# Second half's norm moved behind the mixers' first dense products, alternating score heads, and plain-pair loads spread over the last block

## The chip, the cores and the metric

The kernel runs on one core of a Trainium2 chip. The metric is device time in microseconds (us), the median of several executions. A profile of one execution says when each engine worked: PE is TensorE (matrix products), PEld its weight loads, DVE VectorE, ACT ScalarE, POOL GpSimd, and SP the engine that issues most DMA transfers. Each engine takes its instructions from its own queue, in a fixed order. Engines wait for each other through semaphores, and the order within a queue is set when the program is built.

## The reference

One layer over a sequence of 1024 tokens with 1024 channels, in 32-bit floats:

```python
x = x + 0.5 * swiglu_ffn(rms_norm(x, norm_ffn1), ffn1_w_in, ffn1_w_out)      # d_ff = 2816
x = x + token_mixer(rms_norm(x, norm_mix), w_in, w_out, ...)
x = x + 0.5 * swiglu_ffn(rms_norm(x, norm_ffn2), ffn2_w_in, ffn2_w_out)
return rms_norm(x, norm_final)

def rms_norm(x, g):  return x * rsqrt(mean(x * x, -1) + eps) * g
# token_mixer: p = u @ w_in, split by columns into four mixers of 256 channels (4 heads of 64):
#   a pooling mixer, HGRN2 and GLA (gated linear attention in chunks of 64), and RWKV-7;
#   their outputs are concatenated and multiplied by w_out.
# RWKV-7 per head, over the tokens t:
#   S = S * w_t - (S kk_t)(kk_t * a_t)^T + v_t k_t^T ;   o_t = S r_t
#   then a group norm over each head's 64 channels of o, a bonus term and a gate
```

## The kernel before

**Tiles and precision.** A tile is 128 channels (partitions) by 512 tokens, so a half `h` of the sequence has 512 tokens, and `x[n, h]` are the 16 tiles of the residual stream (n = 0 to 7; they live in buffers named `gr` and `gg`). A dense product is made of three products of rounded operands: each operand is split in a high part and the rest. `split` makes the high part on ACT (L177, or L180 when a norm's gain is multiplied in) and the low part on DVE (L178, L181). `wload` fetches weights into `wraw` and splits them in the same way into `whi` (ACT, L145) and `wlo` (DVE, L146). The products are issued by L89; `mm`, `pg`, `px`, `pq`, `py`, `po` are PSUM banks.

**Stages.** ffn1_in (to about 470 us), ffn1_out (to 691), the mixers (to 1421), ffn2_in (to 1807), ffn2_out with the final norm (to 2057). A tile framework orders the instructions of each stage by priority, which is by default the order in which they are written; `tc.cur_priority` lowered by `URGENT` = 80 pulls instructions forward.

**ffn1_out and ffn2_out.** `out_seven` multiplies five blocks of channels with seven products per block instead of eight. A block has four quarters `q`, each with new weights. Two of the 22 row blocks of `w_out` are left over: the *plain pair*. In ffn1_out, after the five blocks, `h_tile` loads four tiles of the hidden layer and splits them, four `wload` calls bring the weights, and 16 products follow (half 0, n = 0 to 7, then half 1), each with six matrix products, the update of `x[n, h]` on DVE (L747) and `norm_tile`: it splits the updated tile, times the gain, into `xs` (L180 on ACT, L181 on DVE), squares it (ACT, L211) and adds the square to a sum `o` (POOL, L212).

**Norm of the mixers' input.** `rstd_steps(h)` multiplies the sum of squares with ones (`px<-ones,o`), takes the power -1/2 (DVE L226, POOL L227: `rstok`), and spreads it over the partitions (`px<-ident,rstok`, copied to `rsb`). The dense products can start before, since the row scale is applied to their results.

**Mixers.** `mixers` weaves two kinds of work. A stream of dense jobs (`dense_stream`; for each half `wa`, then `rkv0`, which is the three jobs r, k, v, then `gv` and the others) keeps PE busy. Threads (the norm's `rstd_steps`, constants, four units of RWKV, four group norms, attention levels, gates) yield with a time in us from the table `LAT`; a planner's clock decides after which dense product the next step of a thread is put. That sets PE's order, and each step is traced with lowered priority, so the other engines do it early. Of the attention, the *levels* of HGRN2 alternate PE products `pg<-bdt,gin` with DVE operations (L1542 multiplies, L1547 copies under a mask).

**RWKV units.** A unit has two heads of one half, on partitions 0 to 63 and 64 to 127 of the same tiles. Its scores are 16 products of 64 x 128 by 64 x 128, two instructions each: four groups of four, two groups per head, each group in a bank of `px`, evicted by two masked multiplications on DVE (L1293, L1294). After the unit, `group_norm` (L1387 to L1399) is spawned as a thread.

Of the kernel before, what the change touches and what calls it, by code (L numbers as in the profile page):

```python
# [7 lines left out]
F32 = mybir.dt.float32  # L8
F32R = mybir.dt.float32r
# [7 lines left out]
P = 128  # L17
# [18 lines left out]
           pool=10.0, decay=2.9, rstd=3.0, rstd1=7.0, consts=14.4, rs0=2.8, rs1=4.2)  # L36
# [62 lines left out]
class Thread:  # L99
    def __init__(self, gen, ready=0.0):  # L100
        self.gen, self.ready, self.need = gen, ready, ()


class Trunk:
# [99 lines left out]
    def sumsq_add(self, wk, h, x):  # L204
# [4 lines left out]
        else:  # L209
            t = wk.tile([P, H], F32, name="tmp")  # L210
            nc.scalar.activation(t, x, AF.Square)  # L211
            nc.gpsimd.tensor_tensor(self.sq[h], self.sq[h], t, op=ALU.add)  # L212
# [392 lines left out]
    def out_seven(self, wk, w_out, slot, tmp, blocks, early, acc, after=None):  # L605
# [36 lines left out]
        for i, (b0, nb) in enumerate(blocks):  # L642
# [5 lines left out]
            for q in range(4):  # L648
# [28 lines left out]
                for m, w in zip(self.ORDER7, weights(raw, nb)):  # L677
# [29 lines left out]
                    if last and q == 3 and after is not None:  # L707
                        after(m)
                raw = nraw
            hs = nhs  # L710

    def ffn1_out(self, wk, w_out):
# [17 lines left out]
        def h_tile(f, h):  # L730
# [3 lines left out]

        self.out_seven(wk, w_out, slot, lambda: wk.tile([P, H], F32, name="tmp"),
                       ((9, 2), (1, 2), (3, 2), (5, 2), (7, 2)), (8, 8, 8, 8, 0), acc)
        f0 = 2 * PLAIN
        hs = [[h_tile(f, h) for h in range(2)] for f in (f0, f0 + 1)]
        w = [self.wload([(wo[:, f0:f0 + 2, n * P:(n + 2) * P], 0, None)], 2, 256, 1) for n in range(0, KT, 2)]
        self.norm_new()  # L740
        for h in range(2):
            for n in range(KT):
# [5 lines left out]
                self.norm_tile(wk, "gm", n, h)  # L748

    def ffn2_out(self, wk, w_out):  # L750
# [54 lines left out]
        self.out_seven(wk, w_out, slot, tmp, ((9, 2), (1, 2), (3, 2), (5, 2), (7, 2)), (12, 12, 12, 12, 0), load_acc,  # L805
                       after)
        gf = wk.tile([P, D], F32, name="wrawb", bufs=2)
        nc.scalar.dma_start(gf, self.A["norm_final"].broadcast_to([P, D]))
        self.gf = gf

        def h_tile(f, h):
            t = tmp()
            nc.sync.dma_start(t, self.hd[f, h])
            return self.split(t)

        hp = [[h_tile(f, h) for h in range(2)] for f in (f0, f0 + 1)]
# [65 lines left out]
    def weave(self):  # L882
# [5 lines left out]
        self.threads = [Thread(self.rstd_steps(0), LAT["rs0"]), Thread(self.rstd_steps(1), LAT["rs1"]), Thread(self.ysplit()), Thread(consts, LAT["consts"]), Thread(self.rwkv()), Thread(self.gates())]  # L888
# [26 lines left out]
    def spawn(self, gen, us):  # L915
        self.threads.append(Thread(gen, self.te.clk + us))
# [936 lines left out]
```

## Time and profile before

| | |
|---|---|
| median of three executions | 2061.18 us (2061.09 to 2064.62) |
| the profiled execution | 2059.14 us |
| its span, first to last instruction | 2057.3 us |
| PE / DVE / ACT / POOL busy | 1979.4 / 1541.1 / 964.2 / 442.0 us |
| mean granted PE clock | 0.983 |
| mean DMA rate | 169 GB/s |

A row of an engine's list has the start in us, the duration, the engine, the line of the kernel (L89 is line 89), the operation, what is written and what is read (buffer numbers left out), its shape and how many of the kind follow each other; in square brackets is the idle time before it and what ended it. A row of a group has line, engine, operation and count, then total time and the mean in ns, then idle time in front. A row of stretches has for PE, PEld, DVE, ACT and POOL the busy us with the number of instructions, then the granted PE clock (1.00 is full), the DMA share and GB/s. PE's matrix products overlap each other, so the time that one holds the engine is the distance to the next start.

### The profile page before, as it was taken

Reading aid. Unit: us, or ns where it says so; the run is one execution under the profiler, and the core shown is the slowest. Engines: PE = TensorE matmul, PEld = TensorE weight load, DVE = VectorE, ACT = ScalarE, POOL = GpSimd, SP = SyncE. Lnnn points to the kernel's source line nnn. Section 1 sums busy time; section 2 is a strip of 40 time slices with the busy share of each in tenths; the row PEclk is TensorE's granted clock in tenths of the full one; section 3 lists DMA queues with packets and bytes.
Section 4 is the critical chain, followed back from the end, with each engine's and each line's share of the span. In section 5 each row is a group of like instructions: output and inputs, shape, how many; then the busy total and the mean of one; then the engine's idle time right before and its main releaser. Section 6 shows DMA issues by size and latency. Waiting matters only on the chain. (4 is left out here: it accounts for less than half of the span.)

```text
span 2057.3 us, 29356 instructions
## 1 busy us (share of the span) xinstructions
PE 1979.4 (96%) x10424; PEld 1594.1 (77%) x10424; DVE 1541.1 (75%) x2575; ACT 964.2 (47%) x1801; POOL 442.0 (21%) x449
## 2 busy tenths in 40 slices
PE   7899999999999899989999999999999999999995
PEld 5688888887887678778778787787888887778884
DVE  5868878768878856486576676676978898777786
ACT  7435444544443655343464543444544444444444
POOL 0011110003446602002020010100111222134464
PEclk9999999999999999999999999999999999999998
DMA  8336554457653453333443244655445666786622
GB/s 275 114 93 205 200 189 161 157 186 280 253 203 138 156 159 108 91 92 97 145 147 106 83 140 134 207 172 160 139 162 187 202 211 215 242 289 254 246 89 91
DMA packets 304402, 348.60 MB, mean 169 GB/s; under 512 B 28160, under 2 KB 230240, under 8 KB 304256
## 3 DMA queue, kind: packets, MB, share of 16 engines
q1 hardware_dynamic: 301152, 339.14, 49.8%
q0 software_dynamic: 1664, 4.95, 0.7%
q10 hardware_dynamic: 1440, 2.65, 0.4%
q8 instruction: 82, 1.34, 0.3%
q14 instruction: 64, 0.52, 0.1%
HBM read 234.22 MB, written 112.46 MB: 169 GB/s over the span
## 5 line engine op out<-in xcount | busy, mean ns | idle before, releaser
L89 PE MATMUL mm<-xs,whi 128*128 128x512 f32 x1568 | 521.0, 413 | 10.3 <-ACT xs L177 3.9
L89 PEld LDWEIGHTS mm<-xs,whi 128*128 128x128 f32 x1568 | 287.4, 192 | 81.5 <-issue 8.5
L89 PE MATMUL mm<-xs,wlo 128*128 128x512 f32 x784 | 315.4, 402 | 12.1 <-DVE wlo L146 9.7
L145 ACT CAST whi<-wraw 128x512 fp32r<-128x512 f32 (+1 forms) x192 | 118.1, 620 | 171.7 <-PE mm L89 121.1
L300 ACT CAST whi<-wsum 128x512 fp32r<-128x512 f32 x176 | 108.3, 620 | 179.2 <-PE pq L89 49.4
L89 PEld LDWEIGHTS mm<-xs,wlo 128*128 128x128 f32 x784 | 150.6, 192 | 50.4 <-DVE wlo L146 12.1
L89 PE MATMUL pq<-xs,whi 128*128 128x512 f32 x576 | 181.0, 394 | 2.3 <-ACT xs L177 1.8
L146 DVE TENSOR_TENSOR wlo<-wraw,whi 128x512 fp32r<-128x512 f32 (+1 forms) x192 | 134.3, 707 | 63.2 <-ACT whi L145 51.1
L89 PE MATMUL pg<-xs,whi 128*128 128x512 f32 x560 | 176.9, 395 | 4.7 <-DVE hx L559 2.7
L89 PE MATMUL px<-xs,whi 128*128 128x512 f32 x560 | 175.2, 393 | 1.2 <-DVE xs L178 1.2
L301 DVE TENSOR_TENSOR wlo<-wsum,whi 128x512 fp32r<-128x512 f32 x176 | 121.5, 697 | 28.2 <-ACT whi L300 27.9
L89 PE MATMUL pq<-xe,whi 128*128 128x512 f32 x448 | 139.2, 392 | 0.0
L89 PEld LDWEIGHTS pq<-xs,whi 128*128 128x128 f32 x576 | 108.5, 189 | 27.2 <-ACT xs L177 2.7
L89 PEld LDWEIGHTS pg<-xs,whi 128*128 128x128 f32 x560 | 105.0, 189 | 29.5 <-issue 3.1
L89 PEld LDWEIGHTS px<-xs,whi 128*128 128x128 f32 x560 | 105.2, 188 | 25.9 <-DVE xs L178 2.3
L89 PE MATMUL pq<-xs,wlo 128*128 128x512 f32 x288 | 114.2, 396 | 3.8 <-DVE wlo L301 3.8
L340 POOL TENSOR_TENSOR tmp<-tmp 128x512 f32<-128x512 f32 x22 | 33.1, 1503 | 374.0 <-ACT tmp L330 310.6
L89 PE MATMUL pg<-xs,wlo 128*128 128x512 f32 x280 | 110.3, 394 | 0.0
L89 PE MATMUL px<-xs,wlo 128*128 128x512 f32 x280 | 109.9, 392 | 0.0
L89 PEld LDWEIGHTS pq<-xe,whi 128*128 128x128 f32 x448 | 84.3, 188 | 18.7
L622 ACT CAST whi<-wsum 128x512 fp32r<-128x512 f32 x80 | 49.7, 621 | 95.1 <-PE px L89 25.5
L340 POOL TENSOR_TENSOR gr<-gr 128x512 f32<-128x512 f32 x18 | 36.6, 2031 | 256.7 <-ACT gr L330 198.0
(460 smaller groups left out, 4319.9 us busy)
## 6 DMA issues: line engine op xcount, KB each, us to landing
hs<-hx SPq DMA_DIRECT2D x126, 512.0 KB, 3.4
xs<-hs SPq DMA_DIRECT2D x90, 512.0 KB, 6.5
wraw<-in_ffn_w_in SPq DMA_DIRECT2D x68, 512.0 KB, 4.1
wraw<-in_w_in SPq DMA_DIRECT2D x52, 512.0 KB, 4.1
wrawb<-in_ffn_w_in SPq DMA_DIRECT2D x44, 512.0 KB, 4.6
wraw<-in_ffn_w_out SPq DMA_DIRECT2D x42, 512.0 KB, 3.6
xe<-hs SPq DMA_DIRECT2D x36, 512.0 KB, 7.4
wraw<-in_w_out SPq DMA_DIRECT2D x16, 512.0 KB, 4.1
```

The costliest lines, as they stand in the source:

```text
L89: return self._add(self.nc.tensor.matmul(out, lhsT=lhsT, rhs=rhs, **kw), n * 0.42e-3 if rhs.dtype == F32R else max(n * 1.68e-3, 0.04))
L145: nc.scalar.copy(hi[:, :n], raw[:, sl])
L146: nc.vector.tensor_tensor(lo[:, :n], raw[:, sl], hi[:, :n].bitcast(F32), op=ALU.subtract)
L300: nc.scalar.copy(hi[:, :H], a)
L301: nc.vector.tensor_tensor(lo[:, :H], a, hi[:, :H].bitcast(F32), op=ALU.subtract)
L340: nc.gpsimd.tensor_tensor(kept[5], kept[5], kept[7], op=ALU.add)
L622: nc.scalar.copy(v(hi), src)
```

## The change

It has five parts.

1. *Plain pair, ffn1_out.* `out_seven` calls `late(q)` after each quarter of the last block. There one hidden tile and one piece of weights (256 columns of both row blocks) are fetched and split, with `split` into `xs`, `hx` or `xe` buffers. The four `wload` calls are gone.
2. *Plain pair, ffn2_out.* `late(q)` there fetches and splits one hidden tile per quarter, and the gain of the final norm in the first.
3. *Second half's norm.* In the plain pair `norm_tile` is called for half 0 alone. The first four dense jobs (`wa` and the three of `rkv0`) are wrapped by `with_norm`: after the job's body, two tiles of half 1 go through `norm_tile`, with the squares in `st` buffers and the sum on DVE instead of POOL. After the fourth, `rstd_steps(1)` is spawned (it was a thread from the start).
4. *Scores.* Two visits instead of groups: each has eight products whose heads alternate, one bank for each head.
5. *Group norm.* Threads have a precedence of their own; three of the four group norms get none, so their other engines' work is traced in plain order.

```diff
-            t = wk.tile([P, H], F32, name="tmp")
+            t = self.stile() if wk is None else wk.tile([P, H], F32, name="tmp")
             nc.scalar.activation(t, x, AF.Square)
-            nc.gpsimd.tensor_tensor(self.sq[h], self.sq[h], t, op=ALU.add)
+            (nc.vector if wk is None else nc.gpsimd).tensor_tensor(self.sq[h], self.sq[h], t, op=ALU.add)
...
+                if last:
+                    late(q)
...
+        def late(q):                                   # ffn1_out
+            hs[q // 2].append(h_tile(f0 + q // 2, q % 2))
+            raw = wk.tile([P, H], F32, name="tmp")
+            nc.sync.dma_start(raw.rearrange("p (f c) -> p f c", c=256), wo[:, f0:f0 + 2, 2 * q * P:(2 * q + 2) * P])
+            if q < 3:
+                t = wk.tile([P, 2 * H], F32R, name="hx", bufs=3)
+            else:
+                t = wk.tile([P, 2 * H], F32R, name="xe", bufs=6)
+            hi, lo = self.split(raw, t=t)
+            w.append([(hi[:, f * 256:f * 256 + 256], lo[:, f * 256:f * 256 + 256]) for f in range(2)])
...
-        hs = [[h_tile(f, h) for h in range(2)] for f in (f0, f0 + 1)]
-        w = [self.wload([(wo[:, f0:f0 + 2, n * P:(n + 2) * P], 0, None)], 2, 256, 1) for n in range(0, KT, 2)]
...
-                self.norm_tile(wk, "gm", n, h)
+                if h == 0:
+                    self.norm_tile(wk, "gm", n, h)
...
+        def late(q):                                   # ffn2_out
+            if q == 0:
+                gf = self.gf = wk.tile([P, D], F32, name="wrawb", bufs=2)
+                nc.scalar.dma_start(gf, self.A["norm_final"].broadcast_to([P, D]))
+            t = tmp()
+            nc.sync.dma_start(t, self.hd[f0 + q // 2, q % 2])
+            hp[q // 2].append(self.split(t))
...
+        def with_norm(body, n):
+            def both(w):
+                yield from body(w)
+                for k in (n, n + 1):
+                    self.norm_tile(None, "gm", k, 1)
+                if n == KT - 2:
+                    self.spawn(self.rstd_steps(1), LAT["rs1"])
+            return both
...
+        for i in range(4):
+            self.jobs[i] = (self.jobs[i][0], with_norm(self.jobs[i][1], 2 * i))
...
-        for c2 in range(4):
-            ps = self.px.tile([P, 4, P], F32, name="px")
-            hd = c2 // 2
+        for half in range(2):
+            banks = [self.px.tile([P, 4, P], F32, name="px") for _ in range(2)]
             for i in range(4):
+                for hd, ps in enumerate(banks):
+                    hs = slice(hd * 64, hd * 64 + 64)
+                    te.matmul(ps[:, i], lhsT=bk[hs, 4 * half + i].rearrange("p x t -> p (x t)"),
+                              rhs=rK[hs, 4 * half + i].rearrange("p x t -> p (x t)"), start=True, stop=True)
...
+            if half == 0:
+                yield 2 * LAT["score"]
...
-        self.spawn(self.group_norm(pr, h, O, vt, d2), 0.0)
+        self.spawn(self.group_norm(pr, h, O, vt, d2), 0.0, URGENT if pr and h else 0)
```

The changed file has its lines a little further down: the update L747 is L760 there, the levels' L1542 and L1547 are L1568 and L1573, the group norm's L1387 to L1399 are L1413 to L1425.

The first place is DVE at the end of the plain pair. Before, the first mixer weights (`wlo_6247`, `wlo_6251`, read by job `wa`) stand behind the last updates and splits (`gr`, `gg` are x, `xs` the splits):

```order
L747 SCALAR_TENSOR_TENSOR gg_4324<-mm_6170,gg_4324 128x512
L181 SCALAR_TENSOR_TENSOR xs_6164<-gr_4230,vec_76,xs_6164 128x512
L747 SCALAR_TENSOR_TENSOR gg_4324<-pg_6184,gg_4324 128x512
L181 SCALAR_TENSOR_TENSOR xs_6178<-gg_4324,vec_76,xs_6178 128x512
L146 TENSOR_TENSOR wlo_6247<-wraw_6244,whi_6246 128x512
L146 TENSOR_TENSOR wlo_6251<-wraw_6244,whi_6250 128x512
```

After, DVE at the start of the pair has the same weights (now `wlo_6196`, `wlo_6200`) in the last quarter of the last block, before the first update L760:

```order
L672 SCALAR_TENSOR_TENSOR gr_4322<-pg_5879,gr_4322 128x512
L146 TENSOR_TENSOR wlo_6196<-wraw_6193,whi_6195 128x512
L146 TENSOR_TENSOR wlo_6200<-wraw_6193,whi_6199 128x512
L672 SCALAR_TENSOR_TENSOR tmp_4490<-mm_5878,tmp_4490 128x512
L672 SCALAR_TENSOR_TENSOR gg_4324<-px_5880,gg_4324 128x512
L146 TENSOR_TENSOR wlo_6206<-wraw_6203,whi_6205 128x512
L178 TENSOR_TENSOR xs_5964<-tmp_5962,xs_5964 128x512
L672 SCALAR_TENSOR_TENSOR gr_4322<-pq_5881,gr_4322 128x512
L178 TENSOR_TENSOR xe_5969<-tmp_5967,xe_5969 128x512
L675 TENSOR_TENSOR gr_4322<-gr_4322,tmp_4490 128x512
L760 SCALAR_TENSOR_TENSOR gr_4130<-mm_5972,gr_4130 128x512
```

The weights moved ahead of all 16 updates, and the last splits of hidden tile and weights (`xs_5964`, `xe_5969`) stand among the block's own updates.

DVE at the end of the pair after the change still has the splits of half 1 between the updates, and then the small constants, the last two splits and the mean of the norm (`rstok_6234`):

```order
L760 SCALAR_TENSOR_TENSOR gg_4324<-mm_6131,gg_4324 128x512
L181 SCALAR_TENSOR_TENSOR xs_6421<-gr_4230,vec_76,xs_6421 128x512
L760 SCALAR_TENSOR_TENSOR gg_4324<-pg_6139,gg_4324 128x512
L1048 TENSOR_SCALAR omu_6179<-vec_76 128x8
...
L181 SCALAR_TENSOR_TENSOR xs_6483<-gg_4324,vec_76,xs_6483 128x512
L181 SCALAR_TENSOR_TENSOR xs_6489<-gg_4324,vec_76,xs_6489 128x512
L1056 RECIPROCAL lbr_6185<-lbe_6184 128x2
L226 TENSOR_SCALAR rstok_6234<-px_6229 128x4
```

So half 1's splits kept their place; its squares and sums moved into the jobs.

The second place is PE at the first unit's scores. Before, two groups of one head stand together (`px_6806`, `px_6813`: head 0), the others come one by one between dense products:

```order
L89 MATMUL px_6790<-sel_6399,t_6668 64x2 x8
L89 MATMUL px_6806<-gr_6629,gr_6665 128x128 x4
L89 MATMUL px_6813<-gr_6629,gr_6665 128x128 x4
L89 MATMUL mm_6750<-xs_6053,whi_6700 128x512 x2
...
L89 MATMUL mm_6750<-xs_6081,wlo_6701 128x512
L89 MATMUL px_6829<-gr_6629,gr_6665 128x128 x4
```

After, the two banks, one for each head, alternate in the first visit:

```order
L89 MATMUL px_6783<-sel_6362,t_6651 64x2 x8
L89 MATMUL px_6799<-gr_6615,gr_6648 128x128
L89 MATMUL px_6800<-gr_6615,gr_6648 128x128
...
L89 MATMUL mm_6746<-xs_6035,whi_6696 128x512 x2
...
L89 MATMUL mm_6839<-xs_5993,wlo_6739 128x512
L89 MATMUL px_6856<-gr_6615,gr_6648 128x128
```

Four such pairs make a visit; the second visit (from `px_6856`) stands six dense products of three matrix products each further down, where before two more visits followed.

The third place is DVE at the first unit's group norm, beside the first attention levels. Before, the norm's last rows (`go`) stand in front of the first level's multiply (L1542) and masked copy:

```order
L1395 TENSOR_TENSOR go_8002<-go_8002,gva_8010 128x512
L1236 SCALAR_TENSOR_TENSOR t_8057<-smask_6403,t_8049 128x512
L1397 TENSOR_TENSOR go_8002<-go_8002,lnw_6413 128x512
L1238 TENSOR_TENSOR t_8049<-t_8057,t_8049 128x512
L1399 TENSOR_TENSOR go_8002<-go_8002,go_8003 128x512
L1542 TENSOR_TENSOR gin_7910<-gin_7910,gg_7914 128x256
```

After, the second unit's preparation (L1281 to L1294) and most of the norm stand ahead of that multiply (L1568):

```order
L1282 TENSOR_TENSOR gr_8045<-t_8040,t_8034 128x8x64
L1288 TENSOR_TENSOR gr_8106<-t_8038,t_8042 128x8x64
L1289 TENSOR_TENSOR gr_8106<-t_8102,t_8042 128x8x64
L1294 SCALAR_TENSOR_TENSOR t_8111<-rin_7991,vec_76,t_8102 128x512
L1423 TENSOR_TENSOR go_7995<-go_7995,lnw_6376 128x512
L1568 TENSOR_TENSOR gin_7906<-gin_7906,gg_7910 128x256
L1425 TENSOR_TENSOR go_7995<-go_7995,go_7996 128x512
```

The norm moved back by single rows, and the second unit's rows moved forward past the first levels.

More of the change, by code (lines that the diff above doesn't have):

```diff
@@ L603, in ahead, with out_seven @@
         return hs, steps()
-    def out_seven(self, wk, w_out, slot, tmp, blocks, early, acc, after=None):
+    def out_seven(self, wk, w_out, slot, tmp, blocks, early, acc, late, after=None):
         nc = self.nc
@@ L804, in ffn2_out @@
         f0 = 2 * PLAIN
-        self.out_seven(wk, w_out, slot, tmp, ((9, 2), (1, 2), (3, 2), (5, 2), (7, 2)), (12, 12, 12, 12, 0), load_acc,
[L806 to L816, printed above, removed]
+        hp = [[], []]
+        def late(q):
[5 more added lines that the diff above has]
+            hp[q // 2].append(self.split(t))
+        self.out_seven(wk, w_out, slot, tmp, ((9, 2), (1, 2), (3, 2), (5, 2), (7, 2)), (12, 12, 12, 12, 0), load_acc,
+                       late, after)
         for c in range(2):
@@ L903, in step @@
         te, tc = self.te, self.tc
[L904 to L905 removed]
+        tc.cur_priority -= t.urgent
         r = next(t.gen, self)
[L907 removed]
+        tc.cur_priority += t.urgent
         if r is self:
@@ L1010, in half @@
             return sum((made[n]((h,)) for n in JOBS[h].split()), [])
-        self.jobs = half(0) + [(lambda: None, lambda w: mark())] + half(1)
+        def with_norm(body, n):
[6 more added lines that the diff above has]
+            return both
+        self.jobs = half(0)
+        for i in range(4):
+            self.jobs[i] = (self.jobs[i][0], with_norm(self.jobs[i][1], 2 * i))
+        self.jobs += [(lambda: None, lambda w: mark())] + half(1)
         for n in range(KT):
@@ L1284, in rwkv_unit @@
         mask = lambda o: self.rmask[:, o:o + 64].unsqueeze(1).broadcast_to([P, 4, 64])
[L1285 to L1288 removed]
+        for half in range(2):
+            banks = [self.px.tile([P, 4, P], F32, name="px") for _ in range(2)]
             for i in range(4):
[L1290 to L1296 removed]
+                for hd, ps in enumerate(banks):
+                    hs = slice(hd * 64, hd * 64 + 64)
+                    te.matmul(ps[:, i], lhsT=bk[hs, 4 * half + i].rearrange("p x t -> p (x t)"),
+                              rhs=rK[hs, 4 * half + i].rearrange("p x t -> p (x t)"), start=True, stop=True)
+            for hd, ps in enumerate(banks):
+                ss = slice(8 * hd + 4 * half, 8 * hd + 4 * half + 4)
+                nc.vector.tensor_tensor(Ak[:, ss], ps[:, :, 64:128], mask(64), op=ALU.mult)
+                nc.vector.tensor_tensor(Ar[:, ss], ps[:, :, 0:64], mask(0), op=ALU.mult)
+            if half == 0:
+                yield 2 * LAT["score"]
         AkL = Ak[0:64].rearrange("p (x c) t -> p x c t", x=2)
```

30 lines of the change are left out of this document (10 added, 20 removed).

## The prediction

> **What bounds the kernel now.** I read the busy shares first, then the span cut into stretches, then TensorE's own rows with the gap in front of each.
>
> ```profile
> PE 1979.4 (96%) x10424; PEld 1594.1 (77%) x10424; DVE 1541.1 (75%) x2575; ACT 964.2 (47%) x1801; POOL 442.0 (21%) x449
> core 0: 2057.3 us, clock 0.983
> 650.00:700.00 50.00, 38.67 (x159) 29.04 (x158) 48.68 (x58) 29.94 (x51) 36.67 (x25) 0.96 0.41 148
> ```
>
> TensorE is busy 1979.4 of 2057.3 us, so only 78 us are idle. A change can gain in three ways: fewer TensorE microseconds, fewer gaps, or fewer stretches at half clock (0.983 mean, so 0.017 x 2057 = 35 us of granted clock are missing). In the stretches (columns: length, busy time of PE, PEld, DVE, ACT, POOL, clock, DMA share, GB/s) the changed place, 650 to 700, has PE at 38.67 of 50 and DVE at 48.68: VectorE leads there. The profiled execution took 2059.14 us, 2.0 below the median of 2061.18; I work out differences and take them off the median.
>
> ```profile
> 666.40 0.50 PE L89 MATMUL mm<-xs,whi 128*128 128x512 f32 x1 [2.81 <-ACT xs L177]
> 669.14 0.50 PE L89 MATMUL mm<-xs,whi 128*128 128x512 f32 x1 [0.64 <-ACT xs L177]
> 691.73 0.71 PE L89 MATMUL mm<-xs,whi 128*128 128x512 f32 x2 [0.21 <-DVE gr L747]
> 699.44 0.79 PE L89 MATMUL mm<-xs,wlo 128*128 128x512 f32 x1 [7.00 <-DVE wlo L146]
> 700.03 1.05 PE L89 MATMUL mm<-xs,whi 128*128 128x512 f32 x2
> 702.59 0.62 PE L89 MATMUL mm<-xs,whi 128*128 128x512 f32 x2
> 706.27 0.94 PE L89 MATMUL px<-ones,o 128*128 128x1 f32 x8
> 707.86 1.05 PE L89 MATMUL px<-ident,rstok 128*128 128x128 f32 x8
> 708.67 0.70 PE L89 MATMUL mm<-xs,whi 128*128 128x512 f32 x2
> ...
> 680.24 0.68 DVE L747 SCALAR_TENSOR_TENSOR gr<-mm,gr 128x512 f32<-128x512 f32 x1
> 680.84 1.18 DVE L181 SCALAR_TENSOR_TENSOR xs<-gr,vec,xs 128x512 fp32r<-128x512 f32 x1
> 681.95 0.68 DVE L747 SCALAR_TENSOR_TENSOR gr<-pg,gr 128x512 f32<-128x512 f32 x1
> 698.70 2.36 DVE L146 TENSOR_TENSOR wlo<-wraw,whi 128x512 fp32r<-128x512 f32 x2
> 700.99 0.74 DVE L181 SCALAR_TENSOR_TENSOR xs<-gg,vec,xs 128x512 fp32r<-128x512 f32 x1
> ...
> 675.02 11.57 POOL L212 TENSOR_TENSOR o<-o,tmp 128x512 f32<-128x512 f32 x7 [6.16 <-ACT tmp L211]
> ```
>
> Before the plain pair TensorE waits 2.81 + 0.64 us for the splits of the h tiles. In the pair each of 16 products costs DVE one L747 and one L181, 1.71 us from one L747 to the next (680.24 to 681.95). TensorE needs less and follows. The first mixer weights' wlo stands behind all of that at 698.70: a gap of 7.00, then half clock (two products 1.05, later 0.62). L181 takes 1.18 beside POOL's L212 and 0.74 without (700.99).
>
> **First stage.** No plain-pair weight passes ACT and DVE after the last block any more; its splits stand in the block's four quarters. Are they covered there?
>
> ```profile
> 653.75:663.60 9.85, 9.85 (x43) 7.66 (x41) 9.71 (x12) 3.32 (x6) 9.69 (x7) 1.00 0.18 60
> ```
>
> In the last of the four quarters PE is full and DVE busy for 9.71 of 9.85 us. Two L178 more in each (about the 0.7 of an L181 alone, 1.2 beside POOL) overfill such a quarter by 1.3 to 2.3 us. The weights' own wlo run some 4 us ahead of their products by my walk down DVE's queue, so I cost this at nothing; with that cover gone it would be up to 3.
>
> So the 3.4 us of waits go. I walked the new queues with these durations: eight first-half tiles still at 1.7, the eight second-half tiles at about 1.26 (0.60 from L747 to L181, then 0.66: the 0.74 of L181 alone less the same overlap of 0.08; POOL is now idle there. The second half's L181 still stand between the updates). TensorE enters wa at about 687.5 instead of 691.73, and whi and wlo are already there: the 7.00 and about 1.5 of half clock are gone. wa takes 24 x 0.23 + 0.8 (first ones products), ending near 694. Then comes a new stall, the rstd chain:
>
> ```profile
> 702.02 1.28 ACT L1030 ACT_TABLE_LOAD   x1 [3.16 <-DVE lbe L1029]
> 705.22 1.03 POOL L227 TENSOR_TENSOR rstok<-rstok,mhalf 128x4 f32<-128x4 f32 x1 [1.57 <-DVE lbr L1031]
> ```
>
> DVE's last update is at about 691.8; behind it stand small constants, a reciprocal that needs ACT's table (1.28 + 0.2), the mean, POOL's power (1.03), then eight rstok products (0.8). The second job starts at about 695.8 instead of 708.67, 12.9 earlier. The second half's ones products (706.27, 0.8) are only moved behind it, so 12.1. What it puts later: seven adds of 0.65 and eight squares in the first four jobs. DVE has there per job two wlo (0.69), raw and st (0.7 each) and two adds, 4.1 of 5.5 us, so it fits, with a ring of three st tiles that I cost at 0.2. The rest, 0.4, is for the DVE backlog. Stage: 11.5 gained; ends 8 and 13.
>
> **Scores.**
>
> ```profile
> L89 PE MATMUL px<-gr 64*128 64x128 f32 x128 | 17.6, 283 | 0.0
> 1044.82 2.05 PE L89 MATMUL px<-gr 64*128 64x128 f32 x16
> 1046.79 0.79 PE L89 MATMUL mm<-xs,whi 128*128 128x512 f32 x2
> 1054.72 1.16 PE L89 MATMUL px<-gr 64*128 64x128 f32 x8
> 1055.80 0.73 PE L89 MATMUL mm<-xs,whi 128*128 128x512 f32 x2
> ...
> 735.34 1.13 PE L89 MATMUL px<-rin,w2a 64*128 64x512 f32 x4
> 736.40 0.39 PE L89 MATMUL mm<-whi,xs 128*128 128x272 f32 x1
> 749.50 1.98 PE L89 MATMUL px<-raw,glaw 16*128 16x512 f32 x4
> 751.41 0.74 PE L89 MATMUL mm<-xs,whi 128*128 128x512 f32 x2
> ```
>
> A unit's 32 instructions come in visits of 16, 8 and 8. From each start to the next product's they hold TensorE 1.97 + 2 x 1.08 = 4.1 us; four units 16.5. Solving 1.97 and 1.08 for 16 and 8 gives 0.11 an instruction and about 0.2 a visit. Do two heads on rows 0 to 63 and 64 to 127 run together? The w2a products do exactly that, on both halves of the rows: four of 512 columns take 1.06, against 1.91 for four that share their rows (factor 0.555). The new order makes 16 pairs in two visits: 16 x 0.11 + 2 x 0.2 = 2.2 a unit, 1.9 less, 7.6 in all. Scaling by the 0.555 gives 16.5 x 0.445 = 7.3; I take 7.5. Ends: 0 (weight loads of 128 columns don't overlap) and 8.5. Both banks must be free at once; the second visit stands 3 to 4 us behind the first, time for four evictions of 0.42, and I cost that at nothing (0.5 a unit if DVE is late).
>
> **Half clock.**
>
> ```profile
> 757.20:760.60 3.40, 3.40 (x10) 2.16 (x8) 2.26 (x6) 3.35 (x4) 0.00 (x0) 0.50 0.27 99
> 1047.30:1050.70 3.40, 3.40 (x9) 2.19 (x9) 1.53 (x5) 3.36 (x6) 0.18 (x1) 0.50 0.00 0
> 1095.10:1102.00 6.90, 6.90 (x70) 6.28 (x67) 3.10 (x6) 2.46 (x7) 0.00 (x0) 0.51 0.18 46
> ```
>
> In two of four units the clock falls to 0.50 for 3.4 us right after the first score visit, although PE was busy throughout; the same happens in the inversions (1095.10). Small products evidently count as little activity. Each 3.4 us at half clock costs 1.7. A visit of 1.1 instead of 2.0 should spare one of the two: 1.5 gained, between 3.4 and a loss of 3.4, because a start 12 us earlier moves the inversions against these stretches.
>
> The Trainium skill, "TensorE: Matmul & The Clock Gate", Part 1, has the clock halved after an idle window of about 3.4 us, on a window that runs freely. The 7.00 gap agrees; the row at 757.20, with no idle time before it, shows more than that page's rule does. By the page alone this part would be zero.
>
> **Group norm without precedence.**
>
> ```profile
> 888.42 2.04 PE L89 MATMUL pg<-bdt,gin 128*128 128x128 f32 x8 [6.38 <-DVE PT L1547]
> 882.67 0.69 DVE L1395 TENSOR_TENSOR go<-go,gva 128x512 f32<-128x512 f32 x1 [1.53 <-POOL gva L1394]
> 885.60 0.69 DVE L1399 TENSOR_TENSOR go<-go 128x512 f32<-128x512 f32 x1
> 886.20 0.42 DVE L1542 TENSOR_TENSOR gin<-gin,gg 128x256 f32<-128x256 f32 x1
> ```
>
> This is the largest mixer gap: 6.38, then 1.16 at 896.87, with about 1.9 of half clock. The first level's L1542 waits behind the norm's rows. In the new order they still stand among the level's rows, and unit 1's preparation now comes ahead of the second level; my walk gives gaps of 3.6 and 3.9. Net zero; ends 2 gained and 3 lost.
>
> **The end.**
>
> ```profile
> 2008.26 0.66 PE L794 MATMUL px<-ident,gr 128*128 128x128 f32 x4 [1.03 <-ACT xe L796]
> 2008.92 2.87 DVE L178 TENSOR_TENSOR xs<-hx,xs 128x512 fp32r<-128x512 f32 x2
> 2013.64 0.33 PE L794 MATMUL px<-ident,gr 128*128 128x128 f32 x1 [0.92 <-DVE gr L675]
> ```
>
> Gaps of 1.03 and 0.92 stand beside four L178 that now come in the block's quarters; one of them, in the last quarter, may bring 0.7 back. Gain 1.2, ends 0 and 2.
>
> **Sum.** 11.5 + 7.5 + 1.5 + 0 + 1.2 = 21.7. I take 1.7 off for small new waits in a stage with reordered queues (the mixers have a dozen gaps of 0.3 to 1.6 now). 20 gained: 2061.2 - 20 = 2041.
>
> **Rivals.**
> - *Heads don't run together.* 7.5 and the 1.5 of clock are lost: 2050. For it: each score also loads 128 columns of weights. Against: the four w2a products load as many. Chance 0.10.
> - *The mixers give some back:* group norm's rows and half clock fall badly, 3 + 3.4 lost instead of 1.5 gained: 2049. Chance 0.15.
> - *DVE still paces the whole pair:* the first half's adds last on POOL, so L181 stays at 1.18 in the second half as well; 8 x 0.45 (1.71 against 1.26) = 3.6 less: 2045. Chance 0.10.
> - *Slower: each change of head empties the array.* The place is the scores, the price the visit's 0.2 at every instruction instead of every burst. The other terms gain 12.7 less 1.7; the scores would have to cost 11 more than their 16.5, 27.5 / 128 = 0.21 us an instruction, for no change. At 0.11 + 0.2 = 0.31 they cost 40, 23 more, and the time is 2073. The w2a rows speak against it. Chance 0.04.
>
> The forecast itself has 0.55; 0.06 is left for unseen waits that eat all. 0.2% (4 us) is about what a measurement can tell from no change. Faster: 0.55 + 0.10 + 0.15 + 0.10 less 0.01; same 0.05; slower 0.06. The range goes from all upper ends but one (13 + 8.5 + 3.4 + 2, 2034) to the scores' rival with 2 more, 2052.
>
> **What would show it.** Right: no gap above 1 us before the plain pair, wa entered without a wait for wlo, a gap of about 1 us at rstok, score visits of about 1.1 us, eight of them. Wrong: a gap for wlo in the last block's quarters, score visits of 1.9 us, new half-clock stretches between 700 and 1250, or gaps over 4 us at pg in the first unit's attention levels.

## The result, and the profile after

The changed kernel takes 2076.66 us (median of 4 runs, 2072.49 to 2078.87) where the kernel before, on the same chip, takes 2062.45 (4 runs): ratio 1.0066, 95% interval 1.0045 to 1.0086. It is slower by 14 us; 20 us faster was forecast, and 2052 was the upper end. The profiled execution took 2074.88 us (before: 2059.14).

The busy shares and the core's row of after, the stretch 650 to 700, and then the mixers as one stretch, from the first to the last `rstok` product, after first and before second (columns as in the prediction):

```profile
PE 1981.7 (96%) x10424; PEld 1596.1 (77%) x10424; DVE 1547.1 (75%) x2582; ACT 964.7 (47%) x1801; POOL 432.0 (21%) x442
core 0: 2072.8 us, clock 0.979
650.00:700.00 50.00, 46.33 (x201) 35.47 (x200) 47.09 (x75) 27.79 (x45) 34.88 (x31) 1.00 0.48 159
697.80:1436.40 738.60, 702.85 (x4878) 562.80 (x4878) 473.16 (x943) 334.66 (x670) 80.57 (x183) 0.96 0.42 126
```

```profile
707.90:1421.70 713.80, 697.47 (x4871) 557.86 (x4869) 467.06 (x936) 330.64 (x664) 80.74 (x184) 0.98 0.44 130
```

The stretch 650 to 700 did what it was to do: PE from 38.67 to 46.33 busy microseconds of 50, the clock from 0.96 to 1.00. The mixers start 10.1 us earlier, and then take 738.6 us instead of 713.8. What follows them, up to the end of the span, takes 636.4 instead of 635.6. So +24.8 - 10.1 + 0.8 = 15.5, the difference of the two spans: the whole loss is in the mixers.

TensorE's rows with the gaps, at the end of ffn1_out and at the mixers' start:

```profile
642.47 0.73 PE L89 MATMUL pq<-xs,whi 128*128 128x512 f32 x2 [1.31 <-ACT tmp L668]
654.12 0.73 PE L89 MATMUL pq<-xs,whi 128*128 128x512 f32 x2 [1.67 <-ACT tmp L668]
672.18 1.66 PE L89 MATMUL mm<-xs,hx 128*128 128x512 f32 x6 [1.28 <-DVE gr L760]
697.84 1.16 PE L89 MATMUL px<-ident,rstok 128*128 128x128 f32 x8 [0.51 <-POOL rstok L227]
698.75 0.70 PE L89 MATMUL mm<-xs,whi 128*128 128x512 f32 x2
```

The 2.81, 0.64 and 7.00 us are gone. In their place stand 1.31 and 1.67 in the last block's quarters, for ACT (which has the new splits to do there; that they are what makes it late is argued, not shown), 1.28 in the pair and 0.51 at the rstd chain. A little later, at 734.01, TensorE waits 2.00 us more for ACT (`gat`, L1201). That wait is also in e2 and e11 below, which have part 3, and is missing in before and in e3, which has not. The scores:

```profile
747.65 2.08 PE L89 MATMUL px<-gr 64*128 64x128 f32 x14 [1.03 <-DVE n L1303]
756.11 1.16 PE L89 MATMUL px<-gr 64*128 64x128 f32 x16
757.20 0.73 PE L89 MATMUL mm<-xs,whi 128*128 128x512 f32 x2
```

Sixteen instructions hold TensorE for 1.09 us (756.11 to 757.20), against 1.97 in before. The second visit of each unit takes that long. The first visits take longer: 1.41 us in two units, 2.33 in a third, at half clock, and 3.52 in the unit above, where the visit waits 1.03 us for its second bank, which DVE has to read out first (`n`, L1303), and runs at half clock (2.08).

Now the mixers' new gaps. TensorE's largest ones, then SP's queue of after around the first of them, then SP's queue of before at the same place:

```profile
881.68 1.16 PE L89 MATMUL pg<-bdt,gin 128*128 128x128 f32 x8 [2.76 <-ACT bdt L1546]
888.64 2.05 PE L89 MATMUL pg<-bdt,gin 128*128 128x128 f32 x8 [4.42 <-DVE gin L1568]
940.53 2.04 PE L89 MATMUL px<-go,g 128*128 128x512 f32 x2 [6.38 <-DMA go<-pd_xg]
1052.63 1.86 PE L89 MATMUL px<-sel,t 128*64 128x2 f32 x16 [4.02 <-DVE st L1223]
...
927.05 0.32 SPq L1121 DMA_DIRECT2D pd_xg<-st  x1
936.96 0.45 SPq L1460 DMA_DIRECT2D xd<-t  x1
937.51 0.54 SPq L1127 DMA_DIRECT2D go<-pd_xg  x1
```

```profile
930.54 0.32 SPq L1096 DMA_DIRECT2D pd_y<-gin  x1
930.91 0.42 SPq L1102 DMA_DIRECT2D go<-pd_xg  x1
938.43 0.46 SPq L1434 DMA_DIRECT2D xd<-t  x1
```

In before the load of `go` is issued at 930.91, ahead of the store `xd`, which has to wait for POOL until 938.43. In after the two have changed places. The store of the data that `go` loads was issued at 927.05, but the load stands behind `xd` until 937.51, and TensorE waits 6.38 us. None of the change's five parts touches either transfer.

All gaps in the mixers together, their length less PE's busy time, are 35.8 us (16.4 in before). Half-clock stretches in the mixers sum to 61.4 us (34.1), the scores hold TensorE for 13.0 us (16.7). If each microsecond in which TensorE worked at half clock is counted as half a microsecond, the mixers are 710.4 us long in after and 697.6 in before. So of the 24.8 us some 13 are waits, less what the scores gained, and some 12 are half clock. (19.4 of gaps less 3.7 of scores give 15.7; the 3 between are not assigned.) I call this length "at full clock" below; it is worked out, not measured.

These 12 us belong to this pair of executions, and to the mixers alone. Outside the mixers after has 25.0 us at half clock and before 37.2. And the clock differs from run to run: the profiled execution of before had 0.983, but the 106 runs of before beside the experiments below have 0.979 on average, at a mean of 2065.3 us. After's four runs have 0.9775 (standard error 0.0012) at a mean of 2076.2. At the 1.56 us for 0.001 that is worked out at the end, this difference of the clocks is worth 3 us of the 11. Most of the loss is waits, and e9 below shows the same.

### The profile page after: what moved, and what is told of

It reads as the page before. It is cut to its first block, busy times and chain, and to the rows that moved or that the text cites. A ratio compares the mean times of both kernels' runs of the same rounds, so it can differ in the third digit from the quotient of the medians.

```text
span 2072.8 us, 29360 instructions
## 1 busy us (share of the span) xinstructions
PE 1981.7 (96%) x10424; PEld 1596.1 (77%) x10424; DVE 1547.1 (75%) x2582; ACT 964.7 (47%) x1801; POOL 432.0 (21%) x442
## 5 line engine op out<-in xcount | busy, mean ns | idle before, releaser
L89 PE MATMUL mm<-xs,whi 128*128 128x512 f32 x1536 | 511.5, 414 | 10.5 <-ACT gat L1201 4.4
L89 PEld LDWEIGHTS mm<-xs,whi 128*128 128x128 f32 x1536 | 282.0, 193 | 78.7 <-issue 8.2
L89 PE MATMUL mm<-xs,wlo 128*128 128x512 f32 x768 | 308.8, 402 | 6.2 <-DVE wlo L146 3.6
L89 PE MATMUL pg<-xs,whi 128*128 128x512 f32 x528 | 166.5, 395 | 3.7 <-DVE hx L559 2.7
L89 PEld LDWEIGHTS pg<-xs,whi 128*128 128x128 f32 x528 | 99.3, 189 | 26.7 <-issue 3.1
L89 PE MATMUL pg<-xs,wlo 128*128 128x512 f32 x264 | 104.3, 395 | 0.0
```

The source lines that it names most:

```text
L89: return self._add(self.nc.tensor.matmul(out, lhsT=lhsT, rhs=rhs, **kw), n * 0.42e-3 if rhs.dtype == F32R else max(n * 1.68e-3, 0.04))
```

## Experiments

Each was timed beside the kernel before on the same chip. "Clock" is the mean granted clock over all runs of the kernel; the kernel before had 0.979 beside e1 to e14. "Mixers", "full" and "half" are of the one profiled execution: their length, that length at full clock, and the half-clock time in them.

| run | kernel | median us | ratio to before | clock | mixers / full / half us |
|---|---|---|---|---|---|
| before | | 2061 to 2066 | 1 | 0.979 | 713.9 / 697.6 / 34.1 |
| after | all parts | 2076.66 | 1.0066 [1.0045, 1.0086] | 0.9775 | 738.6 / 710.4 / 61.4 |
| e1 | part 5 undone | 2073.36 | 1.0031 [1.0012, 1.0051] | 0.9767 | 738.6 / 705.0 / 75.1 |
| e2 | part 4 undone | 2061.70 | 0.9995 [0.9968, 1.0023] | 0.9812 | 723.3 / 705.6 / 37.5 |
| e3 | part 3 undone | 2081.36 | 1.0079 [1.0052, 1.0107] | 0.9762 | 738.1 / 707.7 / 66.3 |
| e4 | part 1 undone | 2079.80 | 1.0062 [1.0035, 1.0089] | 0.9749 | 743.3 / 708.7 / 75.1 |
| e5 | planner's wait 3.8 | 2071.23 | 1.0026 [1.0006, 1.0046] | 0.9769 | 738.6 / 701.1 / 78.5 |
| e6 | heads alternate, three visits | 2071.79 | 1.0021 [1.0002, 1.0040] | 0.9769 | 734.0 / 704.1 / 64.9 |
| e7 | two visits, heads in turn | 2081.94 | 1.0057 [1.0033, 1.0080] | 0.9759 | 745.9 / 713.1 / 75.1 |
| e8 | before + e6's scores | 2071.68 | 1.0038 [1.0016, 1.0061] | 0.9761 | 740.2 / 696.9 / 92.2 |
| e9 | two visits at before's places | 2064.74 | 1.0000 [0.9986, 1.0015] | 0.9777 | 726.1 / 697.4 / 61.4 |
| e10 | e9, part 5 undone | 2059.42 | 0.9981 [0.9962, 1.0000] | 0.9797 | 730.1 / 695.9 / 71.7 |
| e11 | parts 4 and 5 undone | 2054.04 | 0.9943 [0.9920, 0.9965] | 0.9843 | 712.3 / 701.5 / 23.9 |
| e12 | before + e9's scores | 2070.67 | 1.0031 [1.0012, 1.0051] | 0.9745 | 724.3 / 694.4 / 61.4 |
| e13 | e12, heads in turn | 2071.35 | 1.0027 [1.0011, 1.0043] | 0.9767 | 725.8 / 698.9 / 58.0 |
| e14 | e10, heads in turn | 2065.21 | 0.9994 [0.9977, 1.0011] | 0.9803 | 728.8 / 701.8 / 58.0 |

Part 2 has no run of its own; its place is read from the rows of after in the next section.

**One part undone each.** e1 gives the group norm its precedence back:

```diff
-        self.spawn(self.group_norm(pr, h, O, vt, d2), 0.0, URGENT if pr and h else 0)
+        self.spawn(self.group_norm(pr, h, O, vt, d2), 0.0)
```

> The changed kernel with all four group norms traced with precedence again (part 5 undone). Theory A (the reordered mixers lose through moved queue positions, whose cause is the scores' part): the load of xg for the first half's second group norm still stands behind the inversion's store xd in SP's queue, so the 6.4 us gap at px<-go,g stays and the time is 2070 to 2080. Rival B (the group norm's lost precedence makes the gaps): the gaps at pg and px<-go,g shrink to those of before and the time is about 2060.

It measured 1.0031: some 7 us back, and the 6.4 us gap is still there (6.28 at 945.61), as theory A has it. So the swap in SP's queue is not part 5's doing.

e2 writes the scores as before (four banks in turn, `yield LAT["score"]` after the second and third; the lines between are left out):

```diff
-        for half in range(2):
-            banks = [self.px.tile([P, 4, P], F32, name="px") for _ in range(2)]
...
-                yield 2 * LAT["score"]
+        for c2 in range(4):
+            ps = self.px.tile([P, 4, P], F32, name="px")
...
+            if c2 in (1, 2):
+                yield LAT["score"]
```

> The changed kernel with the scores of before (part 4 undone). Theory A: the score visits cost 7.5 more, but xg's load stands ahead of xd again, so the 6.4 us gap and about 3 us of half clock behind it go, and other steps return to their places: 2062 to 2072. Rival B (group norm) or rival C (the first stage's shift by 10 us moves everything): the gaps stay and 7.5 is lost: about 2084.

It measured 0.9995, some 15 us back, with theory A: the scores, which were to gain 7.5, cost the most. The 6.38 gap is gone, and half clock is down from 61.4 to 37.5 us.

e3 puts the norm of the second half back into the pair, and its `rstd_steps(1)` back among the threads from the start, with before's waiting time. e4 puts the plain pair's loads behind the last block. A part of each diff:

```diff
-                if h == 0:
-                    self.norm_tile(wk, "gm", n, h)
+                self.norm_tile(wk, "gm", n, h)
...
```

> The changed kernel with the second half's norm whole in the plain pair and its reduction a thread from the start (part 3 undone). Rival C (the norm's adds and squares in the first jobs, with the earlier start, cause the mixers' new waits and half-clock stretches): the first stage loses some 7 us and the later stages win 15 or more back, 2065 or less. Theory A: the mixers keep their gaps and the first stage loses 5 to 9: 2080 to 2086.

```diff
+        late = lambda q: None
...
+        hs = [[h_tile(f, h) for h in range(2)] for f in (f0, f0 + 1)]
+        w = [self.wload([(wo[:, f0:f0 + 2, n * P:(n + 2) * P], 0, None)], 2, 256, 1) for n in range(0, KT, 2)]
```

> The changed kernel with the plain pair of ffn1_out loaded and split after the five blocks, as before (part 1 undone). By the trace the part's gain is the 3.4 us of waits ahead of the pair, and its price the two gaps of 1.3 and 1.7 us for ACT's half of the bank in the last block: 2073 to 2078 if only this counts. Rival C (every shift of the mixers' start throws the clock and the queues about): more than 4 us away from 2076 to either side.

TensorE's rows of e3 at the mixers' start, and those of e4:

```profile
701.06 1.05 PE L89 MATMUL px<-ones,o 128*128 128x1 f32 x8 [3.15 <-POOL o L212]
704.28 2.08 PE L89 MATMUL px<-ident,rstok 128*128 128x128 f32 x8 [0.95 <-POOL rstok L227]
```

```profile
664.76 0.57 PE L89 MATMUL mm<-xs,whi 128*128 128x512 f32 x1 [2.27 <-ACT xs L177]
698.13 1.16 PE L89 MATMUL px<-ident,rstok 128*128 128x128 f32 x8 [2.45 <-POOL raw L1168]
```

Without part 3 the first `rstok` product comes at 704.28 instead of 697.84, for a wait of 3.15 on POOL's sums. Without part 1 it comes at 698.13, about the same as with it, and neither kernel has the 7.00 gap for wlo: each of the two parts alone takes that gap away. In the times (1.0079 and 1.0062 against 1.0066) neither differs from after by more than the intervals; rival C, which asked for a large change in either, is not borne out. Part 3 is thus seen in the rows only, and part 1 brings nothing that can be measured beside it.

**The scores taken apart.** e5 changes the planner's wait alone, until the order of `go` and `xd` is again that of before:

```diff
-                yield 2 * LAT["score"]
+                yield 3.8
```

> The changed kernel with the scores' one wait set to 3.8 in place of 3.4 in the planner's table of times; nothing else. In the first half's second unit this puts the inversion one or two dense products later and xg's load ahead of xd's store in SP's queue again; the other steps stay within one product. Theory A1 (that one flip is most of the loss): the gap of 6.4 at px<-go,g goes with its half clock, 8 to 10 less than the changed kernel: 2066 to 2069. Theory A2 (the loss is spread over many places where the planner's positions moved): 3 to 7 less, 2070 to 2074. Rival (part 4's products themselves are the harm): no change, 2076.

1.0026: some 8 us of the 14 are back, from one number in the planner. The 6.38 gap is gone, and at full clock the mixers are 9.3 us shorter (701.1 against 710.4). The ratio fits theory A1 and the median theory A2, so the two are not told apart; the rival, no change, is out. e6 keeps the heads alternating but in three visits, of 16, 8 and 8 instructions, where before has them; e8 makes the same edit in the kernel before and nothing else (the lines of the loop's body are left out):

```diff
+        for c0, n in ((0, 4), (4, 2), (6, 2)):
+            banks = [self.px.tile([P, 4, P], F32, name="px") for _ in range(2)]
...
+            if c0 < 6:
+                yield LAT["score"]
```

> The changed kernel with heads alternating in three visits (8, 4 and 4 products) at the places and with the waits of before, so that every other step of the mixers stands where it stood before. Theory A (moved positions are the loss, the overlap is a gain): the time of the run without part 4 (2062) less the overlap, 6 to 8: 2054 to 2056. Rival (alternating heads do harm by themselves, by two banks held or by small products in a shorter time): 2062 or more.

> The kernel before with nothing but heads alternating in its own three visits, all positions as before. Theory A: faster by the overlap and a little half clock after the visits, 6 to 9: about 2055 against 2062.5. Rival (small products in a shorter time bring half clock, or DVE is late with four evictions a visit): within 3 us of before.

The group of the scores in e8 (total us and mean ns, then the idle time before), and its largest gap:

```profile
L89 PE MATMUL px<-gr 64*128 64x128 f32 x128 | 14.7, 322 | 6.6 <-DVE gr L1296 6.3 <-DVE n L1278 0.3
1067.79 1.85 PE L89 MATMUL px<-gr 64*128 64x128 f32 x8 [4.01 <-DVE gr L1296]
```

The products fall from 17.6 to 14.7 busy us, but two banks are needed at once, and the visits wait 6.3 us for masks that DVE has not yet done. e8 is slower than before by 0.38% with nothing else changed. e6 measured 1.0021: back from 1.0066, but slower than e2, which differs from it in the scores alone (0.9995). So the gain of 6 to 9 us that theory A expected of the two is not there, and the rival's reading holds: alternating heads in before's three visits do harm. At full clock both are a little shorter than their partners (704.1 against 705.6, 696.9 against 697.6); the mean clock is lower (0.9769 against 0.9812, 0.9761 against 0.979).

e7 keeps after's two visits and only runs the heads one after the other:

```diff
-            for i in range(4):
-                for hd, ps in enumerate(banks):
-                    hs = slice(hd * 64, hd * 64 + 64)
+            for hd, ps in enumerate(banks):
+                hs = slice(hd * 64, hd * 64 + 64)
+                for i in range(4):
```

> The changed kernel's two visits with the planner's positions as changed, but in each visit the four products of one head stand ahead of the four of the other, so that they run one after the other. Theory A: the loss stays and the overlap's 7 come on top: 2082 to 2085. Rival (the alternation is the harm): the time falls to 2062 to 2068.

1.0057 against 1.0066: no difference beyond the intervals. The time neither rose by the overlap's 7 us nor fell to that of before, so neither theory holds: running the heads together or in turn changes little here.

**All other steps where they were.** In e9 the two visits stand at before's first and third place, and the planner's clock is charged so that every other step keeps its place. The traces show that it does on TensorE: its 4,750 other instructions of the mixers come in exactly the order of e2. In after, 1,822 of the 2,938 that are not of dense products stand one to four dense products away from their place in e2. e10 undoes part 5 in addition, e11 undoes parts 4 and 5 together (the diffs of e1 and e2), and e12 puts e9's scores into the kernel before. e9's lines:

```diff
-                yield 2 * LAT["score"]
+                yield LAT["score"]
+                te.clk += 4 * P * 1.68e-3
+                yield LAT["score"]
+            else:
+                te.clk -= 4 * P * 1.68e-3
```

> The changed kernel with its two alternating visits at the first and third place of before, and the planner's clock charged as before, so that all other steps stand behind the same dense products as before. The second visit then comes six dense products after the first, where both banks are free. Theory A (moved places and banks that aren't free ate the gain): 6 to 7 under the run without part 4 (2062): 2055 to 2057, and no gap over 1.2 us at the scores. Rival D (alternation brings half clock by itself, as the clock of the run on the kernel before, 0.976, suggests): 2062 to 2070 with a mean clock under 0.979.

> The same with all group norms traced with precedence (part 5 undone as well). If the lost precedence costs 2 to 3 here as it did in the changed kernel: 2 to 3 less than the run with the two visits at before's places; if not, within 2 of it.

> The changed kernel without parts 4 and 5: only the loads and the norm are changed against before. The first stage's 10 us stay until 1030 in the run without part 4 and are lost later; if the group norm's precedence is where, 2055 to 2058; if the loss is half clock in the later inversions, about 2061.

> The kernel before with nothing but the two alternating visits at its first and third place, all else where it was. Theory A: 6 to 7 faster than before. Rival D (half clock comes with the alternation): within 3 of before or slower, with a mean clock 0.002 or more below that of before.

e9 is at 1.0000: with the planner's displacement gone, 14 us come back by the ratios (11.5 by the two means). The mean clock is the same as after's (0.9777 and 0.9775), and at full clock the mixers are 13.0 us shorter (697.4 against 710.4). So what came back are waits and not half clock. Theory A's gain over e2 is missing all the same, and two visits still wait for their second bank (1.03 and 3.63 us); the time and the clock are those of rival D. e11 is the version that beats both kernels, 0.9943 [0.9920, 0.9965], 11 us faster than before. Its core row and its mixers:

```profile
core 0: 2047.8 us, clock 0.986
698.40:1410.80 712.40, 694.29 (x4879) 555.81 (x4879) 471.59 (x943) 334.06 (x670) 80.39 (x183) 0.98 0.43 130
```

Its mixers start 9.4 us earlier (698.4 against 707.9) and take no longer than before's; the time is 1 us below the first of the two forecasts. That is in part luck: at full clock they are 3.9 us longer (701.5 against 697.6), and 10.2 us less of half clock pays for it. Part 5 costs 0.52% beside before's scores (e2 against e11), 0.35% in the changed kernel, and 0.19% beside e9's (e10), which is within the intervals. Where it costs shows in two rows of e2 that e11 does not have:

```profile
1025.12 0.60 PE L96 MATMUL px<-ident,gat 128*16 128x128 f32 x4 [2.73 <-ACT go L1430]
1039.15 2.07 PE L89 MATMUL px<-gr 64*128 64x128 f32 x8 [2.94 <-DVE n L1303]
```

The first wait is for a copy of the group norm itself (L1430), which comes later without precedence; the second is for DVE.

e12 is the plain test of alternating heads: the same kernel, the same order elsewhere, and products that take less time. It is slower than before by 0.31%. That is rival D's forecast, with its lower clock. At full clock its mixers are 3.2 us shorter (694.4 against 697.6), as e10's are 5.6 shorter than e11's (695.9 against 701.5); the mean clock is lower by 0.0046 and 0.0047. TensorE's other instructions stand in before's order in e12, and in e11's in e10.

**Overlap or grouping?** e13 and e14 are e12 and e10 with e7's diff, so that only the overlap is taken away.

> Kernel before, with the scores in two visits of two banks at its first and third place as in e12, but the two heads one after the other, so that no products run together. It is e12 with the overlap alone taken away. Theory A (running two heads together lowers the granted clock): mean clock back near the 0.979 of before; the products cost 4 us more than in e12; 2064 to 2067. Theory B (it is the grouping that lowers the clock: the second bank of head 0 and all of head 1 moved by 3.4 us, which shifts the masks and the inversion behind them against the dense products): clock stays near e12's 0.9745 and the time is at or above e12's 2070.7, up to 2076.

> The same on the base of e10 and e11 (parts 1, 2 and 3 kept, group norm's precedence as before): two visits at before's first and third place, the heads one after the other. e10, with the heads together, measured 2059.4 at clock 0.9797; e11, with four banks in three visits, 2054.0 at 0.9843. Theory A (overlap lowers the clock): clock near 0.984, time 2054 to 2057. Theory B (grouping lowers it): clock near 0.980, time 2060 to 2065.

The mean clock is 0.9767 with a standard error of 0.0006 in e13 (e12: 0.9745, 0.0008; before 0.979) and 0.9803 (0.0008) in e14 (e10: 0.9797, 0.0007; e11: 0.9843, 0.0008). On the second base theory B holds: grouping alone takes the clock down. On the first it is between the two. The times leave no doubt: both kernels without overlap are slower than their partners with before's four banks (1.0027 against 1, 0.9994 against 0.9943), by 6 and 11 us, and the overlap gives back nothing on one base and 3 us on the other (e10 against e14, intervals overlapping).

One wait of TensorE is in the four kernels that have two visits at before's places and before's group norm (e10 and e12 4.60, e13 3.67, e14 3.73), at the third unit's scores; in before and e11 it is 0.51 and 0.50. DVE's rows of e14 there, then TensorE's, and then the same of before:

```profile
1041.96 0.69 DVE L1226 TENSOR_TENSOR st<-st,raw 128x512 f32<-128x512 f32 x1 [3.06 <-ACT raw L1225]
1045.86 0.42 DVE L1320 TENSOR_TENSOR gr<-px,rmask 128x256 f32<-128x256 f32 x1
1046.19 0.68 DVE L1162 TENSOR_TENSOR st<-mm,rsb 128x512 f32<-128x512 f32 x1
...
1038.63 1.71 PE L89 MATMUL px<-gr 64*128 64x128 f32 x16
1042.90 0.39 PE L89 MATMUL mm<-xs,wlo 128*128 128x512 f32 x1
1047.02 0.70 PE L89 MATMUL mm<-xs,whi 128*128 128x512 f32 x2 [3.73 <-DVE st L1162]
```

```profile
1048.11 0.69 DVE L1201 TENSOR_TENSOR st<-st,raw 128x512 f32<-128x512 f32 x1 [3.02 <-ACT raw L1200]
1052.34 0.68 DVE L1137 TENSOR_TENSOR st<-mm,rsb 128x512 f32<-128x512 f32 x1
...
1050.50 1.25 PE L89 MATMUL px<-gr 64*128 64x128 f32 x8
1053.17 0.70 PE L89 MATMUL mm<-xs,whi 128*128 128x512 f32 x2 [0.51 <-DVE st L1137]
```

DVE waits 3.06 us for ACT, and all four masks of the visit and the evictions of `mm` pile up behind that, until TensorE has no `mm` bank left. But DVE's wait is not the grouping's doing: before has it as well (3.02). DVE sets the pace of this place, and not TensorE. From the first score of this unit to TensorE's first product behind the eviction it takes 8.35 us in before (1044.82 to 1053.17), 8.33 in e11 and e13, 8.39 in e14 and 9.03 in e10 and e12. Before has a second visit of eight instructions done in that time (at 1050.50), and its half clock of 3.4 us from 1047.30 falls there too and costs almost nothing. What a shorter visit saves here is waited away and the instructions that the grouping moved out of it into the last visit still have to be done.

## Why the prediction was wrong, by its own steps

The step that failed most is the last term of the sum, "1.7 off for small new waits in a stage with reordered queues". The mixers' gaps grew by 19.4 us. The price of two banks that must be free at once, put at nothing in the term for the scores, failed with it.

**First stage, 11.5 forecast.** The second job started at 698.75 instead of 708.67, 9.9 earlier where 12.9 was worked out: right in kind, within the ends of 8 to 13 once the moved ones products are taken off. The missing 3 us are the step that called the splits in the quarters covered, "I cost this at nothing; with that cover gone it would be up to 3". The gaps there are 1.31 + 1.67 = 2.98. The cover failed on ACT, not on DVE, whose queue I had walked. The 2.00 us for ACT at 734.01, behind the second job, was not in the forecast either.

**Scores, 7.5 forecast.** The mechanism of the overlap was right: pairs of instructions start 6 to 7 ns apart, one pair every 0.112 us, and the second visits take 1.09 us (the first ones 1.41 and more). The hold fell by 16.7 - 13.0 = 3.7 us in the profiled run, the wait of 1.03 included, and by 5.6 in e12. The step that failed is "Both banks must be free at once ... I cost that at nothing (0.5 a unit if DVE is late)". DVE was late: 1.03 us at one visit in after, 1.03 and 3.63 in e9, and 6.3 us in e8. At the third unit it sets the pace, so that the time saved in the scores is waited away (3.67 to 4.60 us for `mm` in e10 and e12 to e14). No run with two banks at once is faster than its partner with before's scores.

**New waits, 1.7 forecast.** The mixers' gaps grew by 19.4 us. This is the term that was mis-sized most. I had walked DVE's and TensorE's queues but not SP's: one planner wait of 3.4 in place of two of 1.7 moved steps of other threads by one to four dense products, and that was enough to put `xd` ahead of `go`. e9 shows the price: all steps back in their places, with the heads still alternating, takes the ratio from 1.0066 to 1.0000 at the same mean clock.

**Half clock, 1.5 gained forecast, ends ±3.4.** In the mixers 61.4 us instead of 34.1, some 12 us lost in this pair of executions. Over all runs the mean clock makes it some 3 us, which lies at the forecast's end on the side of a loss. I counted the stretches that stood right behind a score visit. Most of the new ones stand elsewhere: in waits of the list above, and in the inversions. Two of after's:

```profile
802.00:812.20 10.20, 10.20 (x74) 8.34 (x72) 4.86 (x14) 3.21 (x7) 0.18 (x1) 0.50 0.01 2
1245.70:1255.90 10.20, 10.20 (x115) 8.67 (x114) 6.84 (x14) 1.53 (x5) 0.00 (x0) 0.50 0.30 87
```

**Group norm, 0 forecast.** Its gaps became 2.76 and 4.42, as "gaps of 3.6 and 3.9" in my walk. But undoing part 5 is worth 4 to 11 us, more than the 3 lost that I gave as the end: the walk stopped at the first unit's levels, and the waits of 2.73 and 2.94 in e2 stand at the second group norm and the third unit. Why the price depends on the scores beside it was not tried.

**The end, 1.2 forecast.** The part after the mixers took 0.8 us more. The gaps of 1.03 and 0.92 became 1.52 and 0.50:

```profile
2022.39 0.66 PE L808 MATMUL px<-ident,gr 128*128 128x128 f32 x4 [1.52 <-ACT xe L810]
2029.18 0.33 PE L808 MATMUL px<-ident,gr 128*128 128x128 f32 x1 [0.50 <-DVE gr L675]
```

The sum is the same within 0.1 us: the wait for DVE became shorter and the one for ACT longer, so nothing was gained. No run takes part 2 away alone.

**Rivals.** "The mixers give some back" was the right one by its place. Of its two means, the group norm does cost, but at other rows, and half clock is the smaller part; the largest, the moved steps, it does not name. It was sized at 8 us, and the forecast missed by 36. Heads do run together, and changing heads does not empty the array. What parts 1 to 3 were to bring, 11.5 + 1.2 - 1.7 = 11.0, is what e11 measured (11), but by luck in part: the end gained nothing, and the mixers' 3.9 us more at full clock were paid for by less half clock.

Of the signs listed for "right", wa was entered without a wait for wlo; the gap at `rstok` was 0.51 us, and four of the eight visits took 1.1 us. Gaps above 1 us did stand before the plain pair, in the last block's quarters, though for ACT and not for wlo. New half-clock stretches and a gap over 4 us at `pg` came as written for "wrong". The second list was the one that decided.

## What to carry to other kernels

An edit that makes one step shorter in a planned, interleaved order should first be tried with every other step held where it was; here that alone was worth 14 of the 25 us between the changed kernel and the best version. Before two resources are taken at once (two banks for two heads), look at who frees them, for the time of that engine's worst delay and not of its mean. And walk every queue that the reordering touches, SP's too: here the load of `go` was issued 0.55 us after the waiting store `xd`, 10.5 us after its own data's store, and TensorE waited 6.38 us for it.

## What the runs showed of the hardware

**The half clock needs no idle time.** 17.1 us of TensorE's time from the same instruction of the first unit's inversion on, in e12 and then in before:

```profile
804.70:821.80 17.10, 17.10 (x153) 13.73 (x151) 7.53 (x16) 4.54 (x10) 0.81 (x2) 0.50 0.17 53
```

```profile
805.60:822.70 17.10, 17.10 (x227) 14.28 (x226) 12.18 (x28) 7.40 (x17) 0.81 (x2) 1.00 0.21 64
```

TensorE is busy throughout in both; before gets 227 matrix instructions through, e12 153. In each trace all half-clock stretches begin on one grid of 3.413 us, which lies differently in each execution. I counted what TensorE streamed in each grid window of all 16 profiled executions: the columns of each instruction that starts in it, times the share of the array's rows and columns that it uses (the fullest window has 8,192). After a window at full clock with under 1,500 such columns the next was at half clock in 62 of 62 cases; with 1,500 to 2,500 in 101 of 168; with 2,500 to 3,500 in 44 of 325; with 3,500 to 4,000 in 2 of 326; above 4,000 in 0 of 8,294. Of these 209 drops 52 came after windows in which TensorE was busy throughout; in the other windows it stood idle for a part, so waits bring half clock as well. The Trainium skill, "TensorE: Matmul & The Clock Gate", Part 1, names a free-running window of 3413 ns, and that agrees; it speaks of idle windows, and these rows show windows without idle time, so here the measurement decides. Windows at half clock are followed by half clock at about the same counts (121 of 125, 86 of 134, 25 of 76, 2 of 32 and 0 of 60). Since a window at half clock streams about half as much, it is likely that a stretch also feeds itself; that is argued from these counts, not shown by a run.

**The clock is most of the spread between runs.** Over 248 runs, each taken against its own kernel's mean, a lower mean granted clock goes with a longer time, with a correlation of 0.92 and a slope of 1.56 us for 0.001. The 0.0046 that e12 loses against before are 7.2 us, and 7.0 us is what their mean times differ by (2071.9 and 2064.9).

**What stays open.** Why the grouping lowers the clock is not settled. At the first unit's inversion half clock is seen in 0 of the 3 profiled kernels with before's scores and in 12 of the 13 others (one execution each). But counted on the length at full clock, averaged over all positions of the grid, the mixers have 2.2 windows under 1,500 columns in before and 2.8 in e12, 2.5 in e11 and 3.3 in e14. These are hardly more, while after, with its waits, has 5.6. The waits explain after's half clock so far; for e12 to e14 the count is too coarse, and how long a stretch lasts once begun (17.1 us at the row above) was not tried by itself.
